# Turning the normed rows of two token tiles from SBUF, and storing them turned

## The chip, the cores and the metric

The kernel runs on one NeuronCore of a Trainium2 chip. Its engines each run their own instruction stream in order: TensorE (PE, with its weight loads shown as PEld), VectorE (DVE), ScalarE (ACT), GpSimd (POOL) and SyncE (SP). DMA transfers are issued in this kernel from SP's and from ACT's streams (SPq and ACTq in the profile). The metric is the device time of one launch in microseconds (us); lower is better.

## The reference

The reference is one decoder layer in float32 on 2048 tokens of width 1024:

```
hn   = rms_norm(x, mix_pre_g);  proj = hn @ w_in            # q, k, v and the conv input
attn = sliding_window_attention(q, k, v)                     # window 128, 8 heads, sinks, bias
conv = swish(layer_norm(depthwise31(glu(u)))) @ w_conv_pw
h    = x + rms_norm(concat(attn, conv) @ w_out, mix_post_g)
hn   = rms_norm(h, ffn_pre_g)
out  = h + rms_norm((silu(hn @ w_gate) * (hn @ w_up)) @ w_down, ffn_post_g)   # inner width 2816
```

The change concerns the second `hn`: the rows normed ahead of the feed-forward products. The rows lie with a token on each partition; the products need them turned, with a channel on each partition.

## The kernel before

**Tiles and stages.** Tokens are cut into four tiles (0 to 3) of 512. In the trace a buffer's name carries its stage and tile group behind an @: A is the input projection, B attention, C the convolution, U a folding of two weight matrices, W the output projection and both norms around the residual sum (four row blocks of 128 tokens in one tile), H the making of the feed-forward operands, F the gate and up products, G the down product. Tiles 0 and 1 go through H, F and G as one pair, tiles 2 and 3 as another; each pair is multiplied by a scheme of seven block products in place of eight, so H makes seven operands for a pair: B11 (tile 2i, channel blocks 0 to 3), B21 (the same tile, blocks 4 to 7), B22, and the sums T1 to T4. Every float32 operand is split in a high part (a cast by ACT, or by `split_f` at L792) and a low part (a subtraction on DVE or POOL), and each product takes three matmuls of the parts.

**The step that is changed.** `norm_w` (L747) ends a W stage. It adds the residual, stores h, and then an ACT pass per row block writes the normed rows into the buffers `xs` (tag "chl", five buffers, 4 KB a partition), which ACT's queue stores to the DRAM tensor `hn_scr` (L783). `load_cols` (L786) later reads from there, for one channel block k, the four 128x128 blocks of a tile, in pieces of 512 bytes; `turned` (L806) turns them on PE by four transposes against the identity (L810) into one bank of PSUM. `stage_h_plain` (L824) makes B11 and B21 in this way for tiles 0 and 2: an ACT pass with the gain from the bank (`ct`, one bank) to a buffer of tag "gb" (two buffers; L830), a store of it to `hT` by ACT's queue (L831), an ACT cast (L833) and a DVE subtraction. `stage_h_sums` (L837) reads `hT` again, and the columns of tiles 1 and 3 from `hn_scr`, for the other five operands.

**What sets the order.** The main line of the program is a generator run by `run`; beside it lanes (`lb`, `lc`, `lw`, `lh`, `lf` and others) hold generators for other stages. Each yield states an estimated time, and the lanes advance by that time and their rates. The order in which instructions are written is their priority; a planner with a simulated timeline of its own then fixes each engine's order and the buffers, and an instruction whose inputs are ready in that simulation can be put far ahead of the place where it was written. On the chip every engine keeps that fixed order. `lh` holds B11 and B21 of tile 0 (`stage_h_plain`), then tile 1's norm, then the sums. `until(name)` writes out the rest of a lane up to that name at once. `stage_w` (L693) for tile 1 computes the first half of its channels, then runs eight F products (`ready`), loads its second group of operands (`acts(gi + 1)`, four tiles of tag "chl", cast at L708) after the fourth of them, and goes on. For the second pair, `lw` holds C2, W2, C3, W3 and B11.2 in turn, beside the G stage of the first pair.

Of the kernel before, what the change touches and what calls it, by code (L numbers as in the profile page):

```python
# [12 lines left out]
F32 = mybir.dt.float32  # L13
# [4 lines left out]
AF = mybir.ActivationFunctionType  # L18
# [7 lines left out]
P = 128  # L26
T = 512
NT = S // T
KC = D // P
# [8 lines left out]
def layer_kernel(ctx, tc, x, xT, cols, rows, sinks, relb, onehot, w_in, w_pw, w_out, w_gate, w_up, w_down, out):  # L38
    nc = tc.nc
# [4 lines left out]
    dr = ctx.enter_context(tc.tile_pool(name="dr", bufs=1, space=DRAM))  # L44

    uid = [0]
    lab = ["X0"]
# [7 lines left out]
    def t_(tag, shape, dt=F32):  # L55
        return sb.tile(list(shape), dt, tag=tag, name=nm(tag), bufs=BUFS[tag])

    def f4(tag, shape=(P, D)):
        return t_(tag, shape)

    def f2(tag, shape=(P, T)):
        return t_(tag, shape)

    def hl(tag):
        return t_(tag, (P, 2, T), F32R)

    def sm(n, dt=F32):
        kind = "A" if lab[0][0] == "G" else lab[0][0]
        return sb.tile([P, 8], dt, tag="sm" + kind, name=nm("sm"), bufs=16)[:, 0:n]

    def bank(tag, bufs):
        return ps.tile([P, T], F32, tag=tag, name=nm(tag), bufs=bufs)
# [3 lines left out]
    ct = lambda: bank("ct", 1)  # L76


    act = nc.scalar.activation
# [54 lines left out]
    def weight(src, low, made, raw=None, on_pool=True):  # L134
        if raw is None:
            raw = t_("raw", (P, 2, T))
            nc.sync.dma_start(raw, src)
        return [split_w(raw[:, n], "w", low[n], made, on_pool) for n in range(2)]
# [5 lines left out]
    def rsqrt(ssq, n, mean_over, beside_taps=True):  # L144
        v = sm(n)
        y = sm(n)
        t = sm(n)
        vts(v, ssq, 1.0 / mean_over, EPS, ALU.mult, ALU.add)
        vts(y.bitcast(I32), v.bitcast(I32), 1, None, ALU.logical_shift_right)
        vts(y.bitcast(I32), y.bitcast(I32), -1, 0x5F3759DF, ALU.mult, ALU.add)  # L150
        for _ in range(3):
            if beside_taps:
                ptt(t, y, y, ALU.mult)
                ptt(t, t, v, ALU.mult)
                nc.gpsimd.tensor_scalar(t, t, -0.5, 1.5, ALU.mult, ALU.add)
                ptt(y, t, y, ALU.mult)
            else:
                vtt(t, y, y, ALU.mult)
                stt(t, v, -0.5, t, ALU.mult, ALU.mult)
                stt(y, t, 1.5, y, ALU.add, ALU.mult)  # L160
        return y
# [32 lines left out]
    ident = cst.tile([P, P], F32, name="ident")  # L194
# [16 lines left out]
    g_ffn = colt[:, 8:16]  # L211
# [29 lines left out]
    glu_scr = dr.tile([4, P, S], F32, name="glu_scr")  # L241
    hn_scr = dr.tile([S, D], F32, name="hn_scr")
    y_scr = dr.tile([4, P, S], F32, name="y_scr")
    qs = {}
    started = set()

# [433 lines left out]
    def block_half(acc, units, n, first, L, bank_of, s0=0):  # L680
        cs = slice(n * T, (n + 1) * T)
        for i in range(len(acc)):
            s = i + s0
            lab[0] = L
            o = bank_of()
            three(o, [((a[s // 4][:, 0, ss(s)], a[s // 4][:, 1, ss(s)]), (w[:, 0], w[:, 1])) for a, w in units])
            if first:
                act(acc[i][:, cs], o, AF.Copy)
            else:
                vtt(acc[i][:, cs], acc[i][:, cs], o, ALU.add)  # L690
            yield 0.65 * len(units)

    def stage_w(w, atag, htags, rtags, bank_of, norm=None, ready=None):  # L693
        G = KC // len(htags)
        L = f"W{w}"
        lab[0] = L
        acc = [f4(atag) for _ in range(4)]

        def acts(gi):
            aa = []  # L700
            lab[0] = L
            n = 4 if rtags[gi] == "yt" else 2
            for c in range(G * gi, G * gi + G, n):
                ms = t_(rtags[gi], (P, n, T))
                nc.sync.dma_start(ms, mixT[c : c + n, :, w * T : (w + 1) * T].rearrange("c p t -> p c t"))
                for j in range(n):
                    a = hl(htags[gi])
                    act(a[:, 0], ms[:, j], AF.Copy)  # L708
                    vtt(a[:, 1], ms[:, j], a[:, 0].bitcast(F32), ALU.subtract)
                    aa.append([a])  # L710
            return aa

        def weights(gi, n):
            ws = []
            for c in range(G * gi, G * gi + G, 2):
                if c < 4:
                    ws += weight(w_out[c : c + 2, :, n * T : (n + 1) * T].rearrange("c p t -> p c t"), lo_out[n, c : c + 2], w > 0, on_pool=False)
                else:
                    for j in range(2):
                        ws.append(hl("w"))  # L720
                        nc.sync.dma_start(ws[-1].bitcast(F32), fold[n, c - 4 + j])
            return ws

        nxt = acts(0)
        yield W_LEAD
        for gi in range(KC // G):
            aa = nxt
            for n in range(2):
                lab[0] = L
                if n == 1 and gi + 1 < KC // G and not (ready and G * gi + G == 4):  # L730
                    nxt = acts(gi + 1)
                ws = weights(gi, n)
                yield from block_half(acc, list(zip(aa, ws)), n, gi == 0, L, bank_of)
            if ready and G * gi + G == 4:
                for i, c in enumerate(ready()):
                    if i == Q0 // 2:
                        ld.until("C1")
                        lab[0] = L
                        nxt = acts(gi + 1)
                    yield c  # L740
        tail = norm_w(w, acc)
        if norm:
            norm(tail)
        else:
            yield from tail

    def norm_w(w, acc):  # L747
        L = f"W{w}"
        lab[0] = L

        def whole(src):
            t = f4("chl")
            nc.sync.dma_start(t, src)
            return t

        gb = whole(rows[0].partition_broadcast(P))
        ssq = sm(4)
        for s in range(4):
            act(junk, acc[s], AF.Square, accum_out=ssq[:, s : s + 1])
            yield 0.75  # L760
            lab[0] = L
        r = rsqrt(ssq, 4, D, w < 3)
        xs = [whole(x[w * T + s * P : w * T + (s + 1) * P]) for s in range(4)]
        ssq2 = sm(4)
        yield 3
        for s in range(4):
            lab[0] = L
            stt(acc[s], acc[s], r[:, s : s + 1], gb, ALU.mult, ALU.mult)
            yield 1.25
            lab[0] = L  # L770
            vtt(acc[s], xs[s], acc[s], ALU.add)
            r0 = w * T + s * P
            nc.sync.dma_start(h_scr[r0 : r0 + P], acc[s])
            act(junk, acc[s], AF.Square, accum_out=ssq2[:, s : s + 1])
            yield 1.25
        lab[0] = L
        r2 = rsqrt(ssq2, 4, D, w < 3)
        yield 3
        for s in range(4):
            lab[0] = L  # L780
            act(xs[s], acc[s], AF.Copy, scale=r2[:, s : s + 1])
            r0 = w * T + s * P
            nc.scalar.dma_start(hn_scr[r0 : r0 + P], xs[s])  # L783
            yield 1.25

    def load_cols(w, k, tag):  # L786
        t = f2(tag, (P, 4, P))
        nc.sync.dma_start(t, hn_scr[w * T : (w + 1) * T, k * P : (k + 1) * P].rearrange("(s p) c -> p s c", p=P))
        return t
# [14 lines left out]
    COLTAG = {0: ["fc", "at", "fc", "at"], 2: ["fc", "at", "fc", "at"]}  # L804

    def turned(w, k, bank_of, tag):  # L806
        c = load_cols(w, k, tag)
        b = bank_of()
        for s in range(4):
            nc.tensor.transpose(b[:, s * P : (s + 1) * P], c[:, s], ident)  # L810
        return b
# [12 lines left out]
    def stage_h_plain(ws, ops, n, off):  # L824
        L = f"H{ws[0]}"
        for k in range(4):
            lab[0] = L
            b = turned(ws[0], k + off, ct, COLTAG[ws[0]][k] if ws[0] else "fa")
            u = f2("gb")
            act(u, b, AF.Copy, scale=g_ffn[:, k + off : k + off + 1])  # L830
            nc.scalar.dma_start(hT[ws[0] // 2][k + off], u)  # L831
            o = op_tile(ws, ops, n, k, {})
            act(o[:, 0], u, AF.Copy)  # L833
            lo(u, o, False)
            yield 2.0
# [500 lines left out]
    lh = Lane(1.2, 0)  # L1336
# [65 lines left out]
            hn_a[t + 1] += split_x(t + 1, xa[t + 1][0], xa[t + 1][2], range(4, KC))  # L1402
    lw.until("W0")
    mids = [dr.tile([7, NF // 2, P, T], F32, name=f"mids{i}") for i in range(2)]
    hT = [dr.tile([KC, P, T], F32, name=f"hT{i}") for i in range(2)]
    td = dr.tile([4, NF // 2, P, T], F32, name="td")
    keeps = [dr.tile([PRES[2 * i], P, T], F32, name=f"keeps{i}") for i in range(2)]
    ws, ops = (0, 1), {}
# [12 lines left out]
    ws, ops = (2, 3), {}  # L1421
# [76 lines left out]
```

## Time and profile before

| what | value |
|---|---|
| median of 3 runs (lowest, highest) | 1991.65 us (1988.4, 1992.08) |
| the profiled execution's own time; its span | 1988.67 us; 1986.6 us |
| PE, DVE, ACT, POOL busy | 97%, 73%, 48%, 17% of the span |
| instructions | 26669 |
| DMA | 454.56 MB, 229 GB/s mean over the span |

The profiled execution is 2.07 us longer than its span and 2.98 us shorter than the median run. Times in the rows are microseconds from the start of the span. A row of a timeline has a start, a duration, the engine, the line in the kernel, the operation, what it writes and reads, a count, and in square brackets how long the engine stood idle before it and what released it. Lines L85 and L94 are helpers through which all matmuls, and all DVE operations, go, so they are told apart by the names of what they write.

### The profile page before, as it was taken

The page shows a single profiled execution, that of the slowest core. Times are in us where ns is not written, and L with a number is a line of the kernel's source. Part 1 is how long each engine was busy: PE and PEld are TensorE (multiplying, and loading weights), DVE is VectorE, ACT ScalarE, POOL GpSimd, SP SyncE. Part 2 cuts the span into 40 slices and gives each one's busy share as a digit, 9 for nine tenths or more (in the row PEclk, how much of TensorE's full clock was granted, in tenths as well). Part 3 has the DMA queues.
Part 4 walks back from the last instruction along what each step waited for, and adds up shares of the span by engine and source line. Part 5 has one row for each costly group of instructions (what it writes and reads, how often), then busy time and mean ns, then how long its engine had stood idle before and what let it go on. Part 6 is the DMA issues. An engine that isn't in the chain of part 4 may idle for free.

```text
span 1986.6 us, 26669 instructions
## 1 busy us (share of the span) xinstructions
PE 1930.2 (97%) x8730; PEld 1542.3 (78%) x8730; DVE 1460.2 (73%) x2578; ACT 955.2 (48%) x1878; POOL 336.4 (17%) x415
## 2 busy tenths in 40 slices
PE   8999999998999999899999999989999999999997
PEld 6777767776777778778888778768888888888886
DVE  5999969986875898888658975766666665455557
ACT  5455454436737633334355466556634433345443
POOL 4011111003121200000000110144423332311003
PEclk9999999999999999999999999989999999999999
DMA  8797757669659867885477788797844542466664
GB/s 312 253 316 234 228 176 242 213 198 306 203 191 353 290 216 237 285 267 181 154 236 251 266 302 282 270 315 244 289 149 165 170 164 81 143 232 194 210 196 144
DMA packets 229403, 454.56 MB, mean 229 GB/s; under 512 B 22632, under 2 KB 48400, under 8 KB 229264
## 3 DMA queue, kind: packets, MB, share of 16 engines
q1 hardware_dynamic: 211024, 426.64, 64.5%
q10 hardware_dynamic: 18240, 26.22, 3.6%
q8 instruction: 69, 1.13, 0.2%
q14 instruction: 70, 0.57, 0.1%
HBM read 331.65 MB, written 121.12 MB: 228 GB/s over the span
## 4 chain that ended last, share of the span: by engine, by line
PE 43%; DMA 10%; DVE 9%; issue 3%; POOL 2%; ACT 2%; SPq 1%; DVEq 0%; ACTq 0%; POOLq 0%
PE mm@F L85 29%; PE mm@G L85 12%; DVE fc@C L94 2%; PE tr@W L85 2%; DMA gb@F<-keeps 1%; DVE hl@G L94 1%; DMA mids<-fa@F 1%; DMA fa@G<-mids 1%; DMA td<-fc@G 1%; DVE w@F L94 1%; DMA fc@G<-w_down 1%; DMA wx@G<-w_down 1%; DVE fa@F L94 1%; DVE chl@F L94 1%; DMA mixT<-fc@C 1%
## 5 line engine op out<-in xcount | busy, mean ns | idle before, releaser
L94 DVE SCALAR_TENSOR_TENSOR fc@C<-glu@C,colt,fc@C 128x512 f32<-128x512 f32 x480 | 356.5, 760 | 2.9
L85 PE MATMUL mm@F<-hl@H,w@F 128*128 128x512 f32 x1056 | 253.0, 390 | 3.3 <-ACT mm@F L919 2.0
L85 PE MATMUL mm@G<-hl@G,hl@G 128*128 128x512 f32 x924 | 232.6, 397 | 11.2 <-ACT hl@G L792 7.7
L85 PEld LDWEIGHTS mm@F<-hl@H,w@F 128*128 128x128 f32 x1056 | 197.5, 188 | 46.3 <-ACT mm@F L919 3.7
L85 PEld LDWEIGHTS mm@G<-hl@G,hl@G 128*128 128x128 f32 x924 | 173.0, 190 | 51.7 <-ACT hl@G L792 9.0
L85 PE MATMUL mm@A<-hl@A,w@A 128*128 128x512 f32 x840 | 206.5, 395 | 4.2 <-ACT w@A L127 1.9
L792 ACT ACTIVATE w@F<-chl@F 128x512 fp32r<-128x512 f32 x220 | 135.4, 625 | 142.1 <-PE mm@F L85 131.5
L85 PE MATMUL mm@G<-w@G,hl@G 128*128 128x512 f32 x876 | 199.4, 389 | 0.0
L85 PEld LDWEIGHTS mm@G<-w@G,hl@G 128*128 128x128 f32 x876 | 164.4, 188 | 34.1
L85 PEld LDWEIGHTS mm@A<-hl@A,w@A 128*128 128x128 f32 x840 | 155.4, 188 | 42.2 <-ACT w@A L127 2.6
L94 DVE TENSOR_TENSOR w@F<-chl@F,w@F 128x512 fp32r<-128x512 f32 x198 | 144.8, 735 | 35.9 <-ACT w@F L792 35.3
L85 PE MATMUL mm@F<-ql@H,w@F 128*128 128x512 f32 x528 | 128.4, 391 | 9.2 <-ACT mm@F L1026 5.0
L85 PE MATMUL mm@F<-mid@H,w@F 128*128 128x512 f32 x528 | 131.7, 396 | 0.0
L85 PE MATMUL mm@F<-p@H,w@F 128*128 128x512 f32 x528 | 129.4, 390 | 0.0
L85 PE MATMUL mm@F<-x@H,w@F 128*128 128x512 f32 x528 | 125.7, 391 | 0.0
L85 PEld LDWEIGHTS mm@F<-ql@H,w@F 128*128 128x128 f32 x528 | 98.8, 188 | 31.6 <-ACT mm@F L1026 6.4
L494 POOL TENSOR_SCALAR_AFFINE_SELECT p@B<-p@B 128x512 f32<-128x512 f32 x62 | 57.6, 938 | 374.0 <-ACT p@B L492 372.7
L85 PEld LDWEIGHTS mm@F<-mid@H,w@F 128*128 128x128 f32 x528 | 100.0, 190 | 21.9 <-ACT fa@F L1047 0.5
L85 PEld LDWEIGHTS mm@F<-p@H,w@F 128*128 128x128 f32 x528 | 99.5, 188 | 21.0 <-ACT at@F L1040 0.2
L85 PEld LDWEIGHTS mm@F<-x@H,w@F 128*128 128x128 f32 x528 | 98.6, 188 | 21.5 <-issue 0.8
L127 ACT ACTIVATE w@A<-raw@A 128x512 fp32r<-128x512 f32 x110 | 67.4, 625 | 93.5 <-PE mm@A L85 54.8
L94 DVE TENSOR_TENSOR w@G<-raw@G,w@G 128x512 fp32r<-128x512 f32 x73 | 51.5, 705 | 68.1 <-ACT w@G L792 66.8
(302 smaller groups left out, 3300.6 us busy)
## 6 DMA issues: line engine op xcount, KB each, us to landing
mids<-fa@F SPq DMA_DIRECT2D x154, 256.0 KB, 2.8
raw@A<-w_in SPq DMA_DIRECT2D x55, 512.0 KB, 4.7
w@A<-lo_in SPq DMA_DIRECT2D x84, 256.0 KB, 3.6
fc@G<-mids SPq DMA_DIRECT2D x77, 256.0 KB, 3.5
fa@G<-mids SPq DMA_DIRECT2D x75, 256.0 KB, 4.6
gb@F<-keeps SPq DMA_DIRECT2D x72, 256.0 KB, 3.9
w@W<-fold SPq DMA_DIRECT2D x32, 512.0 KB, 5.1
chl@F<-w_gate SPq DMA_DIRECT2D x22, 512.0 KB, 4.1
```

The source lines that it names most:

```text
L85: r = nc.tensor.matmul(*args, **kw)
L94: r = op(*args, **kw)
L127: act(w[:, 0], raw, AF.Copy)
L494: nc.gpsimd.affine_select(out=pg[:, kb].rearrange("p (i q) -> p i q", q=P), in_=pg[:, 1].rearrange("p (i q) -> p i q", q=P), compare_op=AL ...
L792: act(w[:, 0], x, AF.Copy)
```

## The change

For tiles 0 and 2 the normed rows no longer go to `hn_scr`. A new function `turn_row(w, xs, k)` turns channel block k straight from the four buffers `xs`, applies the gain into a "gb" buffer and stores that to `hT`. For tile 0, `xs` is kept in the list `normed`, and `stage_h_plain` calls `turn_row` where it used to load and turn. For tile 2, `norm_w` calls it for all eight blocks as its last step, each with a yield of 2.0, and `stage_h_plain` only loads the turned blocks back from `hT` by SP's queue, into the buffers (tags "fc" and "at") that took the columns before. Ahead of the second group of tile 1's operands stands `lh.until("B21.0")`, since these take the "chl" buffers that `xs` now holds until it is turned. Tiles 1 and 3 keep the way through `hn_scr`.

```
@@ declarations
+    hT = [dr.tile([KC, P, T], F32, name=f"hT{i}") for i in range(2)]     # moved up
@@ stage_w
                     if i == Q0 // 2:
                         ld.until("C1")
+                        lh.until("B21.0")
                         lab[0] = L
                         nxt = acts(gi + 1)
@@ norm_w, last loop and behind it
             act(xs[s], acc[s], AF.Copy, scale=r2[:, s : s + 1])
-            r0 = w * T + s * P
-            nc.scalar.dma_start(hn_scr[r0 : r0 + P], xs[s])
+            if w % 2:
+                r0 = w * T + s * P
+                nc.scalar.dma_start(hn_scr[r0 : r0 + P], xs[s])
             yield 1.25
+        if w == 0:
+            normed.extend(xs)
+        if w == 2:
+            for k in range(KC):
+                turn_row(w, xs, k)
+                yield 2.0
+
+    normed = []
+
+    def turn_row(w, xs, k):
+        lab[0] = f"H{w}"
+        b = ct()
+        for s in range(4):
+            nc.tensor.transpose(b[:, s * P : (s + 1) * P], xs[s][:, k * P : (k + 1) * P], ident)
+        u = f2("gb")
+        act(u, b, AF.Copy, scale=g_ffn[:, k : k + 1])
+        nc.scalar.dma_start(hT[w // 2][k], u)
+        return u
@@ stage_h_plain
-            b = turned(ws[0], k + off, ct, COLTAG[ws[0]][k] if ws[0] else "fa")
-            u = f2("gb")
-            act(u, b, AF.Copy, scale=g_ffn[:, k + off : k + off + 1])
-            nc.scalar.dma_start(hT[ws[0] // 2][k + off], u)
+            if ws[0]:
+                u = f2(COLTAG[ws[0]][k])
+                nc.sync.dma_start(u, hT[ws[0] // 2][k + off])
+            else:
+                u = turn_row(0, normed, k + off)
+                lab[0] = L
             o = op_tile(ws, ops, n, k, {})
             act(o[:, 0], u, AF.Copy)
             lo(u, o, False)
```

More of the change, by code (lines that the diff above doesn't have):

```diff
@@ L1404, in layer_kernel @@
     mids = [dr.tile([7, NF // 2, P, T], F32, name=f"mids{i}") for i in range(2)]
-    hT = [dr.tile([KC, P, T], F32, name=f"hT{i}") for i in range(2)]
     td = dr.tile([4, NF // 2, P, T], F32, name="td")
```

## The prediction

> **What bounds the kernel now.** I read the page's busy shares first, then PE's waits over the whole span, then timelines and windows round the two waits that the change can reach.
>
> ```profile
> PE 1930.2 (97%) x8730; PEld 1542.3 (78%) x8730; DVE 1460.2 (73%) x2578; ACT 955.2 (48%) x1878; POOL 336.4 (17%) x415
> PE mm@G L85 <- ACT hl@G L792: 7.7, 3, 6.5
> PE tr@B L85 <- DVE sm@B L454: 5.6, 1, 5.6
> PE mm@F L85 <- ACT mm@F L1026: 5.0, 2, 3.8
> PE mm@F L85 <- ACT w@F L792: 4.0, 1, 4.0
> ```
>
> PE is busy for 1930.2 of 1986.6 us. The change takes no matmul away, so it can only win from the 56.4 us in which PE stands, and from time at a lowered clock. The two longest single waits, 6.5 and 5.6 us, both lie beside transfers that the change removes.
>
> Gap 1, at 486 us, in the timeline and in windows (columns: window, length, busy time of PE, PEld, DVE, ACT, POOL, then granted clock, DMA share, GB/s):
>
> ```profile
> 476.66 0.38 SPq L607 DMA_DIRECT2D mixT<-fc@C  x1
> 476.84 0.34 ACTq L783 DMA_DIRECT2D hn_scr<-chl@W  x1
> 480.59 0.67 ACTq L783 DMA_DIRECT2D hn_scr<-chl@W  x1
> 483.66 0.55 DVE L94 TENSOR_SCALAR fc@C<-glu@C,colt 128x512 f32<-128x512 f32 x1 [7.43 <-DMA mixT<-fc@C]
> 490.81 0.28 DVE L454 CUSTOM_DVE_ANT_0 p@B<-tr@B,mb@X 128x128 f32<-128x128 f32 x1
> 491.45 1.65 PE L85 MATMUL tr@B<-kz,ql@A 64*128 64x256 f32 x12 [5.59 <-DVE sm@B L454]
> 486.00:492.00 6.00, 0.55 (x4) 0.58 (x6) 5.96 (x18) 1.31 (x4) 0.00 (x0) 0.66 1.03 385
> 492.00:494.00 2.00, 2.00 (x14) 1.64 (x11) 1.96 (x4) 0.88 (x2) 0.00 (x0) 0.50 1.09 368
> 494.00:496.00 2.00, 2.00 (x8) 1.59 (x7) 2.00 (x5) 0.00 (x0) 0.00 (x0) 0.81 1.16 297
> 496.00:498.00 2.00, 2.00 (x10) 1.68 (x9) 2.00 (x8) 0.00 (x0) 0.00 (x0) 1.00 0.30 77
> ```
>
> PE waits for DVE, and DVE is late because a small store, issued at 476.66, frees its buffer only at 483.66. The first and the last of four stores of normed rows (512 KB each) are issued within 4 us of it; the DMA engines are full (share 1.03). After the gap the clock is 0.50 and 0.81 for two windows.
>
> Gap 2, at 1312 us:
>
> ```profile
> 1306.06 0.45 SPq L1102 DMA_DIRECT2D chl@G<-h_scr  x1
> 1308.79 0.67 ACT L830 ACTIVATE gb@H<-ct@H,colt 128x512 f32<-128x512 f32 x1
> 1315.01 0.33 ACTq L831 DMA_DIRECT2D hT<-gb@H  x1
> 1315.38 0.63 ACT L1094 ACTIVATE junk<-p@G 128x512 bf16<-128x512 f32 x1 [5.92 <-DMA chl@G<-h_scr]
> 1317.14 0.61 ACT L792 ACTIVATE hl@G<-mb@G 128x512 fp32r<-128x512 f32 x1
> 1318.33 8.49 PE L85 MATMUL mm@G<-hl@G,hl@G 128*128 128x512 f32 x24 [6.50 <-ACT hl@G L792]
> 1318.30:1320.30 2.00, 1.97 (x5) 1.60 (x6) 2.00 (x3) 2.00 (x5) 2.00 (x2) 0.50 1.08 330
> 1320.30:1322.30 2.00, 2.00 (x6) 1.57 (x5) 1.97 (x4) 1.97 (x7) 1.83 (x4) 0.50 0.69 165
> 1322.30:1324.30 2.00, 2.00 (x6) 1.59 (x5) 1.93 (x4) 1.40 (x4) 2.00 (x4) 0.53 0.86 261
> ```
>
> ACT has the last turned block of tile 2 ready at 1309.46 (1308.79 + 0.67). Its queue issues the store of it only at 1315.01, when another transfer, issued by SP at 1306.06, has landed. ACT stands behind its own store for 5.55 us, and the splits that PE needs stand behind ACT.
>
> **The change part by part.**
>
> *Tile 0, transfers.* Four stores and eight column loads leave (each 2 MB in all), with 3.99 us of SP's queue for the first four loads. The same small store lands elsewhere in 3.8 us:
>
> ```profile
> DMA to landing us min/median/max: 2.3/3.8/5.6
> 489.15 3.99 SPq L788 DMA_DIRECT2D fa@H<-hn_scr  x4
> 478.79 1.14 ACT L781 ACTIVATE chl@W<-x@W,sm@W 128x1024 f32<-128x1024 f32 x1
> 500.72 0.33 PE L810 MATMUL ct@H<-ident,fa@H 128*128 128x128 f32 x1
> 503.95 0.62 ACT L708 ACTIVATE chl@W<-yt@W 128x512 fp32r<-128x512 f32 x1
> 544.94 0.60 PE L810 MATMUL ct@H<-ident,fa@H 128*128 128x128 f32 x4
> 560.17 2.66 PE L85 MATMUL mm@W<-w@W,chl@W 128*128 128x512 f32 x11
> ```
>
> (The first row is for the buffers fc@C from 1100 to 1400 us.) With 3.8 us in place of 7.00, DVE and then PE go on 3.2 us sooner, and the gap shrinks to 2.4 us. The clock windows cost 2 x 0.50 + 2 x 0.19 + 0.55 x 0.34 = 1.6 us of PE's work; I take them as saved too. Term: -4.8 us. Bounds: 0, since DVE is busy throughout the gap (5.96 of 6 us) and the transfers that remain may hold the store as long, and -7.2 (the gap whole, 5.6 + 1.6), which turns of the rows put into the gap would also reach.
>
> *Tile 0, order.* The rows are ready at 479.9, and the turns need not wait for 500.72, so they come sooner; PE, full from 492 on, gains nothing by that. What waits instead: the casts into "chl" (503.95) must now come behind the last turn, at 544.94 if the turns do not move. That leaves 15 us to their first use at 560.17, where four casts of 0.62 us stand ahead. Cost 0; if that cover went, 4 x 0.62 = 2.5 us. The line that writes B21 out early costs nothing as long as the lane is done by then: 16 us of yields at rate 1.2 against 24.8 us of the main line's before it.
>
> *Tile 2, gap 2.* The store at 1315.01 moves away with the block that it carries, as do the last two turns and gain passes. ACT could then go on at 1309.46 and split 5.55 us sooner, leaving PE 0.95 of the 6.50 us. The clock loss after the gap (three windows at 0.50, 0.50 and 0.53, 2.9 us) would go as well: -8.45 us. DMA is still full there, and the next loads are late next: I give 2 us back. Term: -6.5 us. Bounds: 0 and -9.4 (6.5 + 2.9).
>
> *Tile 2, the new place.* Eight turns, eight gain passes and eight stores come behind the norm of tile 2, at about 1175 us, in place of four stores:
>
> ```profile
> 1163.42 0.63 ACT L792 ACTIVATE hl@G<-fa@G 128x512 fp32r<-128x512 f32 x1
> 1170.41 2.19 ACT L781 ACTIVATE chl@W<-mid@W,sm@W 128x1024 f32<-128x1024 f32 x2 [6.36 <-POOL sm@W L156]
> 1175.16 0.63 ACT L792 ACTIVATE hl@G<-mb@G 128x512 fp32r<-128x512 f32 x1 [0.48 <-ACT chl@W L781]
> 1176.37 1.53 PE L85 MATMUL mm@G<-hl@G,hl@G 128*128 128x512 f32 x4 [0.60 <-ACT hl@G L792]
> 1170.00:1180.00 10.00, 9.34 (x40) 7.17 (x39) 4.11 (x8) 9.11 (x14) 0.38 (x1) 1.00 0.82 288
> 1180.00:1190.00 10.00, 9.64 (x44) 7.45 (x43) 5.33 (x10) 5.20 (x10) 0.00 (x0) 1.00 0.94 314
> 1190.00:1200.00 10.00, 10.00 (x45) 8.18 (x45) 3.22 (x11) 5.15 (x9) 2.37 (x12) 1.00 0.89 318
> 1220.00:1240.00 20.00, 20.00 (x95) 16.55 (x94) 12.91 (x21) 13.41 (x25) 0.00 (x0) 1.00 0.92 303
> ```
>
> Here ACT makes no split from 1164.05 to 1175.16, first waiting 6.36 us for the norm on POOL, and PE runs dry for 0.60 us: the lead is just used up. The 32 transposes (8 x 0.60 = 4.8 us of PE, by the row at 544.94) and eight passes (8 x 0.67 us of ACT) only move, so they count 0 over the span. New are two waits: PE's own, for the rows, where ACT alone waited, and those of ACT behind its stores, which hold "gb" and the bank. Lower bound 0: from 1220 to 1240, where two such turns stand today, PE is never idle at a DMA share of 0.92. Upper bound 6.36 + 5.55 = 11.9 us: the norm's wait whole, and one store's as at 1309.46. I take 4 us, nearer the low end, since PE's one dry spell here is 0.60 us and ACT can make up ground after 1180 (5.20 and 5.15 of 10 us busy).
>
> *Tile 2, loads.* SP issues eight loads of `hT` for eight of columns: the same count, 0. Behind a late one, G's loads would queue; the turned stores fall before 1210, so the loads that matter stand behind nothing new. Four "chl" buffers are held longer; ACT's stores and casts for tile 3 come later still, so 0.
>
> *Sum.* -4.8 - 6.5 + 4.0 = -7.3 us on the profiled execution: 1988.67 - 7.3 = 1981.4. The median run was 2.98 us above that one, so for the median I predict 1984.4.
>
> **A rule beside the rows.** The Trainium skill (TensorE: Matmul & The Clock Gate, Part 1: The HAM clock gate) says that PE falls to half its clock after about one idle window of 3.4 us and needs about as long a busy one to return. The two gaps agree: 5.59 and 6.50 us, clock 0.50 behind both. By that rule the 4 us of the new place, as one piece, would add a loss of clock, to be weighed as a rival below; the sum leaves it out.
>
> The Trainium skill (DMA: Bandwidth & Descriptors, Rules for kernel authors) asks for transfers of 1 MiB or more. It speaks against eight stores of 256 KB for four of 512 KB; by it the DMA share at 1170 to 1200 would rise, and the sum come out higher by an unknown part.
>
> **The rivals.**
>
> *ACT's stores at the new place decide (slower).* ACT is busy 9.11 + 5.20 + 5.15 = 19.5 of the 30 us there; eight passes make 24.8, so about 5 us of store waits are free. The change gains 11.3 us elsewhere; it turns slower once the eight stores wait more than 16 us together, 2.0 us each. Store 1315.01 waited 5.55 us. At 3 us each (24 us) PE loses 19 in place of 4: 1984.4 + 15 = 1999. Against it: the windows to 1240 show such stores without a PE wait. Chance 0.24.
>
> *The planner orders something else anew (slower).* New buffer times shift its order downstream; a new wait like those of 3.8 and 4.0 us in the list, twice, with half clock of 1.6 us each, costs 11 us: 1995.8. No row speaks for a place. Chance 0.10.
>
> *Hidden.* DVE's backlog keeps gap 1, and full DMA keeps most of gap 2: half of 11.3 is gained, 4 to 5.5 lost, 1990 to 1992. The same comes out when the new wait is in one piece with a clock loss of 2.9 us and gap 2 keeps 2 us more. Chance 0.13.
>
> *More.* Turns fill what is left of gap 1, gap 2 goes whole, the new place costs nothing: -7.2 - 8.45 = -15.7, 1976. Chance 0.16.
>
> **How the numbers follow.** The forecast has 0.37. A change within 0.2% (4 us) cannot be told from none. Faster: 0.37 + 0.16 = 0.53; same 0.13; slower 0.24 + 0.10 = 0.34. The range must reach both slower cases and nearly the largest gain: 1976 to 2000. The forecast's own range, with 0 to 8 us at the new place, is 1980.4 to 1988.4.
>
> **What would show it.** Right: the stores of rows at 476 us are gone, the small store beside them lands in about 4 us, PE's wait on DVE near 486 is under 3 us with the clock at 1.00 behind it; the wait on the splits near 1312 is under 2.5 us and no ACT store waits there. Wrong: a PE wait over 4 us on the turned bank or on splits between 1165 and 1210, ACT idle ahead of several stores of turned rows, or a gap at 1312 that stays because the split's loads land late.

## The result, and the profile after

The changed kernel takes 2013.98 us (median of 4 runs, 2009.12 to 2014.5) against 1990.84 us for the kernel before in the same comparison. The ratio is 1.0121, with a 95% interval of 1.0107 to 1.0134: it is 1.2% slower, outside the predicted range and on the other side of no change. Its profiled execution took 2014.5 us, with a span of 2012.8 us; the figures below are of that execution, against the span of 1986.6 us of the one before.

The busy shares on the page of the changed kernel:

```profile
PE 1939.7 (96%) x8730; PEld 1549.3 (77%) x8730; DVE 1468.8 (73%) x2578; ACT 952.8 (47%) x1878; POOL 337.4 (17%) x415
```

PE does the same 8730 matmuls and is busy 9.5 us longer, so part of the loss is time at a lower clock (a mean of 0.987 in place of 0.992); it stands still for 73.1 us in place of 56.4. The waits of PE over the whole span (total, times, longest):

```profile
PE mm@F L85 <- ACT mm@F L942: 14.7, 6, 4.1
PE mm@F L85 <- DVE w@F L94: 5.9, 3, 3.5
PE mm@F L85 <- ACT w@F L813: 5.5, 2, 4.0
PE mm@F L85 <- ACT mm@F L1049: 5.1, 3, 3.1
```

The two waits that headed the list before, 6.5 us in G and 5.6 us in B, are both gone. All that heads the list now lies in F, and the largest group waits for "seeds": blocks that ACT casts into the product's bank (L942) after a load from `keeps`.

Where the time went is read from the starts of the same matmul in both traces:

| matmul | before | after | after - before |
|---|---|---|---|
| first F product of tile 0 with "x" | 521.9 | 512.3 | -9.6 |
| 265th F product with "hl" | 721.8 | 722.3 | +0.6 |
| first of G, first pair | 1013.0 | 1016.8 | +3.9 |
| 576th of G | 1223.7 | 1230.1 | +6.4 |
| last of G, first pair | 1342.7 | 1334.2 | -8.5 |
| 265th F product with "x" (second pair) | 1443.2 | 1469.5 | +26.3 |
| last of G with "w", second pair | 1971.1 | 1997.4 | +26.3 |

So 9.6 us are won at the first gap and lost again by 722 us; 15 us are won between 1224 and 1334 us; and 34.8 us are lost in the 100 to 135 us behind that. From 1470 us on the two kernels run alike.

**The first gap.** A window of the changed kernel in its place (columns as in the prediction):

```profile
486.00:492.00 6.00, 6.00 (x27) 4.89 (x28) 6.00 (x15) 3.70 (x7) 0.00 (x0) 1.00 0.73 237
```

PE is busy all through at full clock. What it does there, in the timeline of the changed kernel:

```profile
481.96 0.55 DVE L94 TENSOR_SCALAR fc@C<-glu@C,colt 128x512 f32<-128x512 f32 x1 [6.08 <-DMA mixT<-fc@C]
485.29 1.15 ACT L709 ACTIVATE hl@W<-yt@W 128x512 fp32r<-128x512 f32 x2 [2.28 <-DMA yt@W<-mixT]
486.21 6.65 PE L85 MATMUL mm@W<-w@W,hl@W 128*128 128x512 f32 x28
491.72 0.08 DVE L455 DVE_READ_ACCUMULATOR2_ANT sm@B<- 128x1 f32 x1
494.85 0.97 PE L85 MATMUL tr@B<-kz,ql@A 64*128 64x256 f32 x12
```

and the rows that answer to three of them in the timeline of the kernel before:

```profile
490.69 2.19 ACT L708 ACTIVATE hl@W<-yt@W 128x512 fp32r<-128x512 f32 x4 [4.69 <-DMA yt@W<-mixT]
491.01 0.08 DVE L454 DVE_READ_ACCUMULATOR2_ANT sm@B<- 128x1 f32 x1
493.03 7.45 PE L85 MATMUL mm@W<-w@W,hl@W 128*128 128x512 f32 x28
```

DVE still waits 6.08 us for the small store, and what B needs of DVE comes at 491.72, no earlier than before. PE no longer stands for it, and two things have changed. Tile 1's first W operand, a load of 1 MB that was issued among the stores of normed rows, now lands 5.1 us after its issue (480.18 to 485.27) and not 10.1 us (480.55 to 490.67), so it can be cast at 485.29 in place of 490.69. And the planner has put PE's work in another order: the 28 W matmuls stand ahead of the next twelve of B (494.85), where in the kernel before they stood behind them (491.45, then 493.03). Since PE keeps its fixed order, the earlier load alone would have left it standing for B; which of the two is worth how much, no run separates.

**Tile 2's new place, and C3.** Groups from the views of single buffers: count, shortest, median and longest in ns, and the starts of the first and the last in us. Before:

```profile
L549 PE MATMUL ct@C<-ident,fc@C x16: 270/272/300, 1125.4 to 1187.5; 128*128 128x128 f32 x16
L85 PE MATMUL tr@W<-w@W,chl@W x96: 389/389/397, 1238.7 to 1265.5; 128*128 128x512 f32 x96
L781 ACT ACTIVATE chl@W<-mid@W,sm@W x4: 1133/1135/1154, 1293.4 to 1296.5; 128x1024 f32<-128x1024 f32 x4
```

After (from the views of the buffers: tile 2's turns, what ACT's gain passes waited for, the landing of their stores, and the three rows that answer to those above):

```profile
L801 PE MATMUL ct@H<-ident,chl@W x32: 270/272/330, 1176.0 to 1219.1; 128*128 128x128 f32 x32
...
  PE ct@H L801: 5.5, 5
...
DMA to landing us min/median/max: 2.8/4.2/7.3
...
L550 PE MATMUL ct@C<-ident,fc@C x16: 270/272/273, 1224.4 to 1242.7; 128*128 128x128 f32 x16
L85 PE MATMUL tr@W<-w@W,chl@W x96: 389/389/389, 1297.7 to 1324.2; 128*128 128x512 f32 x96
L783 ACT ACTIVATE chl@W<-mid@W,sm@W x4: 1135/1136/1153, 1350.5 to 1353.6; 128x1024 f32<-128x1024 f32 x4
```

Tile 2's eight turns stand in the one bank `ct` from 1176.0 to 1219.1. C3's four column turns, which go through the same bank and stood at 1125 to 1187, come only behind them, at 1224. With C3 all that needs it is late: the second half of W3 by 59 us (1238.7 to 1297.7) and the normed rows of tile 3 by 57 us (1293.4 to 1350.5). The new stores themselves are harmless: they land in 4.2 us, and the only idle time of ACT ahead of the eight gain passes is for PE's turns, 5.5 us in all.

**What that costs.** Windows before:

```profile
1300.00:1340.00 40.00, 32.59 (x136) 25.52 (x135) 29.70 (x45) 17.93 (x40) 20.64 (x31) 0.87 0.93 314
1360.00:1400.00 40.00, 40.00 (x180) 33.03 (x179) 18.85 (x31) 23.43 (x43) 15.23 (x12) 1.00 0.90 302
1400.00:1440.00 40.00, 40.00 (x185) 32.97 (x184) 31.28 (x41) 26.52 (x48) 18.46 (x13) 1.00 0.85 286
```

and after:

```profile
1300.00:1340.00 40.00, 40.00 (x178) 33.14 (x177) 23.95 (x40) 16.17 (x29) 4.86 (x3) 1.00 0.48 175
1360.00:1400.00 40.00, 30.14 (x116) 22.38 (x114) 29.09 (x52) 17.07 (x41) 19.79 (x23) 0.91 1.01 342
1400.00:1440.00 40.00, 29.45 (x104) 23.07 (x105) 30.58 (x35) 24.99 (x47) 22.12 (x16) 0.79 0.74 250
```

Before, PE stood 7.4 us of 1300 to 1340 and was full behind it. After, it is full there and stands 20.4 us of 1360 to 1440, at clocks of 0.91 and 0.79. In both kernels the bad stretch begins some 20 us behind tile 3's normed rows: PE's first wait of about 1 us or more starts 18 us after 1293.4 before, and 17 us after 1350.5 in the changed kernel. The waits of PE from 1340 to 1445 us, after:

```profile
PE mm@F L85 <- ACT mm@F L942: 9.5, 4, 3.3
PE mm@F L85 <- DVE w@F L94: 5.9, 3, 3.5
PE mm@F L85 <- ACT fa@F L964: 3.1, 2, 2.2
```

**The loss between 614 and 722 us.** Windows before, and then after:

```profile
620.00:640.00 20.00, 18.23 (x87) 14.59 (x85) 8.34 (x13) 13.53 (x23) 0.00 (x0) 1.00 1.02 359
```

```profile
620.00:640.00 20.00, 15.62 (x64) 12.68 (x64) 8.27 (x13) 11.16 (x20) 0.00 (x0) 0.83 1.02 356
```

PE comes there 8 us earlier (613.9 in place of 622.2 for the first F product with "hl"), and stands 4.06 us for the third seed, which ACT casts at 622.93, only 1.4 us earlier than before (624.34). At a mean clock of 0.83 in this window, more of the lead goes: it is 4.0 us at the 25th of these matmuls and 2.6 us at the 37th.

### The profile page after: what moved, and what is told of

It is laid out like the page before. It is cut to its first block, busy times and chain, and to the rows that moved or that the text cites. A ratio compares the mean times of both kernels' runs of the same rounds, so it can differ in the third digit from the quotient of the medians.

```text
span 2012.8 us, 26656 instructions
## 1 busy us (share of the span) xinstructions
PE 1939.7 (96%) x8730; PEld 1549.3 (77%) x8730; DVE 1468.8 (73%) x2578; ACT 952.8 (47%) x1878; POOL 337.4 (17%) x415
## 5 line engine op out<-in xcount | busy, mean ns | idle before, releaser
L85 PE MATMUL mm@G<-hl@G,hl@G 128*128 128x512 f32 x924 | 228.3, 393 | 3.6 <-DVE hl@G L94 2.4
L85 PE MATMUL mm@F<-mid@H,w@F 128*128 128x512 f32 x528 | 140.5, 414 | 18.0 <-ACT mm@F L942 9.5
L85 PEld LDWEIGHTS mm@F<-mid@H,w@F 128*128 128x128 f32 x528 | 105.2, 201 | 43.6 <-ACT mm@F L942 10.7
```

The source lines that it names most:

```text
L85: r = nc.tensor.matmul(*args, **kw)
```

## The experiments

Two questions: which part costs what, and why. For tile 2 three theories were set against each other. **Bank**, later **delay**: the eight turns take `ct` ahead of C3's turns, W3 and tile 3's norm come late, and this is what costs after 1360 us. **Lane**: C3 and W3 are late because the lane `lw` spends 16 units of time on the turns. **Store**: ACT's stores and the two "gb" buffers cost (the prediction's rival). All ratios are to the kernel before on the same chip; two profiles of one and the same kernel below differ by 4.6 us in their last matmul, all of it arisen after 722 us, so such differences of single profiles behind 722 us are not weighed.

**Each part alone.** Tile 0's part alone, against the changed kernel:

```
-            if w % 2:
+            if w:
                 r0 = w * T + s * P
                 nc.scalar.dma_start(hn_scr[r0 : r0 + P], xs[s])
...
-        if w == 2:
-            for k in range(KC):
-                turn_row(w, xs, k)
-                yield 2.0
...
             if ws[0]:
-                u = f2(COLTAG[ws[0]][k])
-                nc.sync.dma_start(u, hT[ws[0] // 2][k + off])
+                b = turned(ws[0], k + off, ct, COLTAG[ws[0]][k])
+                u = f2("gb")
+                act(u, b, AF.Copy, scale=g_ffn[:, k + off : k + off + 1])
+                nc.scalar.dma_start(hT[ws[0] // 2][k + off], u)
```

> Tile 0 as in the change, tile 2's rows and turns as before. Bank theory (all of the loss comes from tile 2's eight turns, which hold the one bank ct ahead of C3's column turns): the stall at 1312 us is back, nothing is lost after 1360 us, and what tile 0 gains at 486 us is given back by 720 us, since tile 1's norm ends at the same time as before; so 1990 to 1996 us, ratio 1.000 to 1.003. My prediction's tile 0 term (-4.8 us kept) gives 1986, ratio 0.9975. If tile 0's part were the cause of the loss: over 2005 us.

Measured: 1993.11 us, ratio 1.0042 (1.0025 to 1.0060). The stall in G is back, nothing is lost after 1360 us, and the 7.7 us won at the first gap have become a loss of 4.5 us at 722 us: tile 0's part costs by itself. The size of that loss varies: in the five kernels here that have tile 0's part and leave tile 1's roots on POOL, the product of 721.8 comes at 721.6 to 726.3. None of them keeps more than 0.2 us of the lead.

Tile 2's part alone, against the changed kernel:

```
-                        lh.until("B21.0")
...
-            if w % 2:
+            if w != 2:
...
-                u = turn_row(0, normed, k + off)
-                lab[0] = L
+                b = turned(0, k + off, ct, "fa")
+                u = f2("gb")
+                act(u, b, AF.Copy, scale=g_ffn[:, k + off : k + off + 1])
+                nc.scalar.dma_start(hT[0][k + off], u)
```

> Tile 2 as in the change, tile 0 as before. Bank theory: most of the 23 us of loss is here, 2005 to 2015 us, ratio 1.007 to 1.012, with the waits between 1360 and 1440 us that the changed kernel has. If the loss needs both parts: below 1996 us.

Measured: 2007.03 us, ratio 1.0093 (1.0073 to 1.0114). The two parts add up within their intervals: 0.42% and 0.93% against 1.21% for both. As the bank theory says, W3's second half comes at 1295.1 and from the end of G to the product that stood at 1443.2 before it takes 134.9 us in place of 100.5, a loss of 34.4 us.

**Other banks.** The whole change, with tile 2's turns in the three banks `tr`:

```
-        b = ct()
+        b = tr() if w else ct()
```

> The whole change with tile 2's eight turns in the three tr banks instead of ct; the lane's order and its 16 units of time, the gb buffers and ACT's stores stay. Bank theory: C3's first turns are back at some 1130 us, W3's second half at about 1240 us, the waits after 1360 us go: 1980 to 1992 us. Lane theory (C3 and W3 come later because the lane spends 16 units on the turns) and store theory (ACT's stores and the two gb buffers space the turns): the loss stays, 2005 to 2015 us. A cost that the bank theory does not count: W3's own products use tr too, and stand behind the turns there.

Measured: 1999.77 us, ratio 1.0059 (1.0039 to 1.0080), above the 1980 to 1992 us of the bank theory, and below what the other two expected. Its groups:

```profile
L801 PE MATMUL tr@H<-ident,chl@W x32: 270/272/328, 1175.3 to 1197.3; 128*128 128x128 f32 x32
L550 PE MATMUL ct@C<-ident,fc@C x16: 270/272/273, 1129.6 to 1191.8; 128*128 128x128 f32 x16
L783 ACT ACTIVATE chl@W<-mid@W,sm@W x4: 1135/1137/1152, 1303.9 to 1307.0; 128x1024 f32<-128x1024 f32 x4
```

C3's turns are back in their old place although lane time, stores and buffers are unchanged, and the loss behind G has gone (from the end of G to the product of 1443.2 it takes 102.3 us, 100.5 before, 135.3 in the changed kernel). What is left is tile 0's part (0.42% by itself) and the cost named beforehand: W3's first half now stands behind the turns in `tr` (it begins at 1199.0 in place of 1147.5), and G ends 10 us later than before, 4.3 us of which it had lost by its start.

The Trainium skill (Perfetto Trace Analysis, section Matmuls) advises rotating independent groups through several banks, so that emptying one overlaps the next group. The traces agree: the eight turns take 22.0 us in three banks and 43.1 us in one.

**Another place.** The whole change with the eight turns given out behind C3 in the same lane; bank, stores, buffers and the 16 units stay:

```
-        if w == 0:
-            normed.extend(xs)
-        if w == 2:
-            for k in range(KC):
-                turn_row(w, xs, k)
-                yield 2.0
+        if w % 2 == 0:
+            normed[:] = xs
...
+    def stage_turns():
+        for k in range(KC):
+            turn_row(2, normed, k)
+            yield 2.0
...
     lw.add("C3", stage_tail(3), lambda: since(lc, "T3", CS))
+    lw.add("H2t", stage_turns())
```

> The whole change with tile 2's eight turns given out in the same lane after C3's tail instead of before it; bank, buffers, stores and the 16 units stay. Bank theory: C3's first three turns come back to 1125 to 1140 us, tile 3's normed rows to about 1300 us, and the loss after 1360 us goes, at least 15 of the 23 us: 1980 to 1998 us. Lane theory: W3 stands behind the same 16 units, so the loss stays, 2005 to 2015 us. Store theory: the same eight stores in the same buffers, 2005 to 2015 us.

Measured: 2006.14 us, ratio 1.0090 (1.0069 to 1.0112); the profiled execution, 2000.39 us, is the fastest of its four. A miss in size for the bank theory: C3's turns did come back (1125.3 to 1181.4), but the time hardly fell. The turns now hold the "chl" buffers until 1266, W3's second half needs these, and all but the first 12 of its 96 matmuls come some 30 us late; tile 3's rows are at 1332.0, and the loss behind G is 24.2 us. So it is not C3's turns in themselves that cost, but what makes tile 3's norm late. From here on I speak of the delay theory.

**No lane time.** The whole change without the time that tile 2's turn loop hands in:

```
                 turn_row(w, xs, k)
-                yield 2.0
```

> The whole change without the 16 units of lane time that tile 2's turn loop hands in; bank, place and stores stay. Lane theory (C3 and W3 are late because the lane spends 16 units on the turns): C3's first turn at about 1130 us, and most of the loss goes, below 2000 us. Bank theory: the eight turns still stand ahead of C3's in the one bank, C3's first turn at 1215 us or later, and the time stays at 2005 to 2018 us.

Measured: 2006.18 us, ratio 1.0090 (1.0073 to 1.0107), with C3's first turn at 1226.4 and tile 3's rows at 1352.3. The lane theory falls: without the 16 units C3 is as late.

**The turns without the change.** The kernel before, with eight turns of tile 2's rows added at the changed kernel's place, their result copied and used by nothing:

```
             nc.scalar.dma_start(hn_scr[r0 : r0 + P], xs[s])
             yield 1.25
+        if w == 2:
+            for k in range(KC):
+                lab[0] = "H2"
+                b = ct()
+                for s in range(4):
+                    nc.tensor.transpose(b[:, s * P : (s + 1) * P], xs[s][:, k * P : (k + 1) * P], ident)
+                act(f2("gb"), b, AF.Copy, scale=g_ffn[:, k : k + 1])
+                yield 2.0
```

> The kernel before, with eight turns of tile 2's normed rows into ct added at the place where the change has them; each is copied to a gb buffer and not stored, and everything else stays, the way through DRAM too. Delay theory: C3's turns come some 45 to 55 us late, W3's second half about 59 us late, tile 3's normed rows at about 1350 us, and the waits between 1360 and 1440 us appear although nothing of tile 2's route has changed: 15 to 35 us above before. And the stall at 1312 us shrinks, if tile 3's norm is what fills that time in the kernel before; it stays at 6 us and more, if it is tile 2's way through DRAM. Store theory (the new stores to hT decide): no store is added, so within 5 us of before.

Measured: 2007.27 us, ratio 1.0107 (1.0078 to 1.0137). Its groups, and its windows:

```profile
L549 PE MATMUL ct@C<-ident,fc@C x16: 270/272/273, 1218.7 to 1237.0; 128*128 128x128 f32 x16
L781 ACT ACTIVATE chl@W<-mid@W,sm@W x4: 1132/1135/1154, 1342.9 to 1346.1; 128x1024 f32<-128x1024 f32 x4
```

```profile
1300.00:1340.00 40.00, 40.00 (x186) 33.02 (x185) 25.56 (x48) 22.44 (x41) 5.72 (x4) 1.00 0.62 226
1360.00:1400.00 40.00, 28.40 (x110) 22.09 (x109) 27.83 (x55) 19.63 (x44) 22.46 (x32) 0.83 1.03 363
```

This kernel stores nothing turned early and sends tile 2's rows through DRAM as ever, yet it loses some 22 us, in the same place. The store theory falls. And the stall of 1300 to 1340 us is gone here too, with tile 2's way through DRAM untouched: that way alone does not make the stall. Tile 3's norm has moved off, and the DMA share of that stretch is 0.62 in place of 0.93.

**Tile 2 without the delay.** Tile 2's part alone, the turns in `tr` and inside W3, behind its first quarter and ahead of the loads that want "chl" (against the kernel with tile 2's part alone):

```
             for n in range(2):
                 lab[0] = L
+                if w == 3 and n == 1 and gi == 0:
+                    for k in range(KC):
+                        turn_row(2, normed, k)
+                        yield 2.0
+                    lab[0] = L
...
         if w == 2:
-            for k in range(KC):
-                turn_row(w, xs, k)
-                yield 2.0
+            normed[:] = xs
+
+    normed = []
...
-        b = ct()
+        b = tr() if w else ct()
```

> Tile 2's part alone (tile 0 as before), its eight turns moved once more: in the three tr banks, and given out inside W3, behind the first of its four quarters and ahead of the loads that want the chl buffers. C3's turns then stand ahead of them, W3's first quarter too. Delay theory (the loss after 1360 us comes only from C3 and W3 being late, so that tile 3's norm falls into pair 2's first products): C3's turns at 1125 to 1190 us, W3's second half at 1235 to 1250 us, no loss after 1360 us beyond 3 us; as to the stall at 1312 us: if it is tile 2's way through DRAM it goes and the time is 6 to 8 us below before (1977 to 1982 at 1985 of before); if it is tile 3's norm and its transfers, it stays and the time is within 4 us of before. If the new stores or turns cost by themselves, wherever they stand: 10 us and more above before.

Measured: 1987.22 us against 1985.71 us, ratio 1.0005 (0.9987 to 1.0023): all of tile 2's loss is gone, and no gain is left. Its rows, windows, and PE's waits over 1 us from 1240 to 1345 us:

```profile
L787 ACT ACTIVATE chl@W<-mid@W,sm@W x4: 1134/1136/1137, 1289.7 to 1292.8; 128x1024 f32<-128x1024 f32 x4
```

```profile
1300.00:1340.00 40.00, 35.35 (x160) 28.28 (x159) 28.63 (x45) 18.84 (x41) 19.82 (x31) 1.00 0.94 318
1360.00:1400.00 40.00, 40.00 (x180) 33.06 (x179) 17.30 (x29) 23.58 (x43) 13.34 (x10) 1.00 0.89 300
1271.99 0.73 PE L85 MATMUL mm@G<-hl@G,hl@G 128*128 128x512 f32 x2 [3.24 <-DVE hl@G L94]
1305.65 11.16 PE L85 MATMUL mm@G<-hl@G,hl@G 128*128 128x512 f32 x48 [2.88 <-DVE x@G L94]
1327.10 3.24 PE L85 MATMUL mm@G<-hl@G,hl@G 128*128 128x512 f32 x13 [1.67 <-DVE hl@G L94]
```

Tile 3's rows are on time, and the F products are full again. The one wait of 6.50 us behind ACT's store is gone together with that store. The four other profiles that keep tile 2's way through DRAM and tile 3's norm on time (tile 0's part alone, and below the same with roots on DVE, twice, and its control) all have it, at 5.77 to 6.13 us. But PE stands as long in sum, 8.4 us from 1240 to 1345 as before, at other waits. For the first, 3.24 us, DVE is busy with tile 3's norm (4.86 us of scaling from 1266.47); the second, 2.88 us, goes back to a load of `w_down` for which ACT waits until 1301.74. From the first to the last G product of the pair it takes 328.9 us, before 329.7 us.

Eight kernels in one table; the last column is the time from the last G matmul of the first pair to the product at 1443.2 before:

| kernel | tile 3's rows normed at | PE idle 1240 to 1345 | PE idle 1345 to 1460 | G's end to F |
|---|---|---|---|---|
| before | 1293.4 | 8.4 | 0.0 | 100.5 |
| tile 2's turns in `tr`, inside W3 | 1289.7 | 8.4 | 1.0 | 101.9 |
| whole change, turns in `tr` | 1303.9 | 7.0 | 1.6 | 102.3 |
| whole change, turns behind C3 | 1332.0 | 3.3 | 15.8 | 124.7 |
| before, with eight idle turns | 1342.9 | 0.0 | 19.0 | 133.0 |
| tile 2's part alone | 1347.9 | 0.0 | 20.7 | 134.9 |
| changed kernel | 1350.5 | 0.0 | 20.4 | 135.3 |
| whole change, no lane time | 1352.3 | 0.0 | 18.5 | 126.7 |

With tile 3's norm late, G stands less and F stands more, and F loses more than G wins. The lateness sets the size only roughly: the last kernel has the latest rows and loses 8.6 us less behind G than the changed kernel.

**Tile 0.** Its win at the first gap is gone by 722 us. In the run with tile 0's part alone, POOL's timeline shows the first inverse root of tile 1's norm mixed with the masks of attention:

```profile
584.95 0.68 POOL L153 TENSOR_TENSOR sm@W<-sm@W 128x4 f32<-128x4 f32 x1 [7.27 <-DVE sm@W L94]
...
588.80 1.67 POOL L495 TENSOR_SCALAR_AFFINE_SELECT p@B<-p@B 128x512 f32<-128x512 f32 x2
...
595.07 0.20 POOL L156 TENSOR_TENSOR sm@W<-sm@W,sm@W 128x4 f32<-128x4 f32 x1
```

It takes 10.3 us, where the kernel before takes 5.0 (593.88 to 598.89), and ends only 3.6 us earlier although it began 8.9 us earlier. So I put both roots of tile 1 on DVE, in the kernel with tile 0's part and, as a control, in the kernel before:

```
-        r = rsqrt(ssq, 4, D, w < 3)
+        r = rsqrt(ssq, 4, D, w in (0, 2))
...
-        r2 = rsqrt(ssq2, 4, D, w < 3)
+        r2 = rsqrt(ssq2, 4, D, w in (0, 2))
```

> Tile 0's part alone, and tile 1's two inverse roots on DVE instead of POOL. Norm theory (the 8 us that tile 0 wins at 486 us are lost at 620 to 720 us because tile 1's norm does not end earlier: its roots took 10.3 us on POOL in place of 4.8 us): the norm's casts come 4 to 9 us earlier than in the run with tile 0's part alone, the seeds behind them too, and the time is 4 to 8 us below that run's. Rival (the transfers are at their limit from 600 to 640 us, share 1.03, and set the pace): the casts come earlier and the time is the same within 2 us.

> The control for the run before: the kernel before with tile 1's two inverse roots on DVE instead of POOL. In the kernel before the roots are done 4.8 us after they start, so both theories expect the same time as before within 3 us; what it differs by is to be taken off the effect in the run with tile 0's part.

Measured: 1982.62 us, ratio 0.9984 (0.9967 to 1.0001), with tile 0's part; 1991.94 us, ratio 1.0027 (1.0015 to 1.0040), for the control. The edit costs 0.3% in the kernel before, where no change was expected, and wins 0.6% with tile 0's part, some 11 us. That is more than the 4 to 8 us of the norm theory, and the way is not the one that it named: the norm's casts begin at 614.9 in place of 617.2, 2.3 us earlier and not 4 to 9. In the changed kernel, with the roots on POOL, they begin at 614.87 too, and the lead is lost all the same. In ACT's timeline of this run a seed stands right behind the casts:

```profile
618.08 1.13 ACT L783 ACTIVATE chl@W<-mid@W,sm@W 128x1024 f32<-128x1024 f32 x1
...
619.12 0.58 ACT L940 ACTIVATE mm@F<-gb@F 128x512 f32<-128x512 f32 x1
```

With the roots on POOL this seed comes at 625.3, behind five more passes and a table load. The new order wins 6 us there, PE waits 0.97 us in place of 4.48, and the order is new because the planner reckons with another engine for the roots. The product of 721.8 comes at 715.6 here, so some 6 us of the lead are kept. That the roots' time on POOL is the cause is therefore not shown; the timelines point to ACT's order of seeds around tile 1's norm, and no run changes that order alone.

The same kernel again, in more rounds:

> The same kernel as tile 0's part alone with tile 1's roots on DVE, measured again in more rounds: 0.9984 of before again, within 0.2%; over 1.000 if the first run's gain was the spread of the runs.

Measured: 1986.10 us against 1988.50 us, ratio 0.9989 (0.9976 to 1.0001): the same again, and no more than a tenth of a percent faster than before.

**The change with one repair, and with both.** The whole change with tile 1's roots on DVE (the edit above, in the changed kernel):

> The whole change as it is, with tile 1's roots on DVE. If tile 0's loss (some 10 us between its part with POOL roots and with DVE roots) and tile 2's loss (the ct bank) are separate, the ratio to before is 1.0121 - 0.0055 = 1.006 to 1.008, some 2000 us at 1986 of before; if the later loss swallows what is won earlier, 1.010 and more.

Measured: 2007.81 us, ratio 1.0100 (1.0084 to 1.0117), where the second expectation begins: the repair for tile 0 wins 0.2% here and not 0.55%. In its profile, that of the fastest of its four runs (2003.67 us), the lead at the end of G is 19.4 us, against 8.5 in the changed kernel, and the loss in F is 34.0 us as ever; what of the lead the other runs keep isn't known.

Both repairs in the changed kernel, the turns in `tr` inside W3 and the roots on DVE, each by the edit shown above:

> Both tiles' turns as the change wants them, with the two costs found so far taken out: tile 2's eight turns in the tr banks inside W3 (as in the run where tile 2 alone was so moved) and tile 1's roots on DVE. If the two parts add up, tile 0's part with DVE roots (0.9984) and tile 2's moved part (1.0005) give 0.999, within 0.3% of before; if tile 2's part had a gain of its own that only the delay of C3 and W3 hid, 6 us and more below before (ratio under 0.997).

Measured: 1980.71 us against 1988.50 us, ratio 0.9967 (0.9954 to 0.9980). This version beats both kernels: 0.33% faster than before, and some 1.5% faster than the change as made. It is 0.22% below the kernel with tile 0's part and DVE roots alone, while tile 2's moved part alone was 0.05% above before; whether tile 2's part wins anything of its own stays open within these 0.2%: the ratio meets both expectations, 0.999 within 0.3% and under 0.997.

## Why the prediction was wrong

**Tile 0, transfers (-4.8, bounds 0 and -7.2).** The gap closed and the clock stayed at 1.00, as said; the win at 521.9 was 9.6 us, beyond the bounds. That the gap closed was luck, for the mechanism was another: the store landed in 5.5 us (476.30 to 481.8), not 3.8, DVE's wait went from 7.43 to 6.08 us, and B's sums came no earlier. What helped was a load that I had not looked at, tile 1's W operand among the stores, cast 5.4 us earlier, and a new order on PE that puts its products ahead of B's. I had asked only what PE waited for, not what else could have run.

**Tile 0, order (0).** This step failed. "PE, full from 492 on, gains nothing by that" left out the way on: what is won must be kept through the next place where other work sets the time. At 619.5 us PE, 8.3 us early, met a seed that ACT cast only 1.4 us earlier than before, and stood 4.06 us for it. Tile 0's part costs 0.42% by itself.

**Tile 2, gap 2 (-6.5, bounds 0 and -9.4).** This step failed in what it took the wait to be worth. The reading of the wait itself holds: where the store has moved away, no wait on ACT's splits of that length is left, and where it stays and tile 3's norm is on time, there is one of 5.77 to 6.13 us. But with tile 3 on time, PE stands the same 8.4 us at other waits, for DVE and for a late load; the prediction gave back 2 us for that. Nor does the store alone make the wait: with tile 2's way through DRAM kept and tile 3's norm late, it goes. So the term is about 0. In the changed kernel G is faster because tile 3's norm has left it; the eight added turns alone do the same.

**Tile 2, the new place (+4.0, bounds 0 and 11.9).** For the place itself the size is about right: PE waited 1.94 us for the first turn, at a clock of 1.00, and lost 2.5 us between 1013 and 1224 us. The sum failed here all the same, and this is the step that made it wrong: it priced the eight turns by PE's and ACT's time and not by the one bank that they hold. "Only move, so they count 0" is true of PE's time and false of `ct`: 43 us of it, ahead of C3 by the order of writing. It delayed tile 3's norm by 57 us and cost 34.8 us in F, of which G gives back some 15: the standing that is gone, a clock of 1.00, and turns that stand elsewhere. I had asked what is late next for SP's loads and for "chl", and not for the bank.

**Tile 2, loads (0).** As said; the "chl" buffers cost nothing in the changed kernel, though they did when the turns were put behind C3.

**The rivals.** The slower one, ACT's stores at the new place, had the right sign and the wrong mechanism: no store was waited for, and eight turns without a store cost the same. Nearest came "the planner orders something else anew"; I gave it 0.10 and 11 us (by its own terms 1995.4, not 1995.8) because no row spoke for a place. There was one: C3's turns in the same bank at 1125 to 1187 us, ahead of the place of the new ones in time and behind it in the order of writing.

**The signs.** None of the signs that were to show the prediction wrong came, and of those that were to show it right only the store's landing failed (5.5 us in place of about 4). They watched the places of the change, and the loss came in F, behind 1360 us.

**The two rules.** By the clock rule that the prediction takes from the Trainium skill (TensorE: Matmul & The Clock Gate, Part 1: The HAM clock gate), a wait of 4 us in one piece at the new place would have cost clock. It was 1.94 us, and the clock stayed at 1.00 from 1170 to 1200. By the rule on transfer size that it takes from the Trainium skill (DMA: Bandwidth & Descriptors, Rules for kernel authors), the DMA share at 1170 to 1200 would have risen. It was 0.45, 0.79 and 0.91, against 0.82, 0.94 and 0.89; only four of the eight stores are issued in these 30 us, so this is a weak test.

**What stays open.** Why the same norm costs F some 35 us and G only some 15 is not settled. The transfers are at their limit from 1360 to 1400 (share 1.01), F's first products need loads of weights and seeds at that time, and the waits are for seeds and weights; ACT's longest wait there, 7.85 us up to 1396.0, ended when a load of weights landed. But no run separates the transfers from the order on ACT and DVE.

## What to carry to other kernels

Price moved work by every resource that it holds, a single bank or buffer ahead of all, and look up who takes that resource next in the order in which the program gives it out, not in the order of the trace. A wait that goes away in the profile is not yet time won: other waits can take its place, or it went for another reason. Add the new work alone, and take the old work away alone. A few microseconds won early are kept only if the next meeting point with another queue moves as well, so follow the lead from stage to stage before it is counted.

## What the runs showed of the hardware

The clock fell without a wait as long as those at the two gaps. Windows of the changed kernel:

```profile
1368.00:1372.00 4.00, 2.58 (x10) 1.80 (x10) 1.76 (x6) 1.31 (x4) 0.24 (x2) 1.00 1.03 385
1372.00:1376.00 4.00, 2.57 (x6) 2.11 (x7) 3.05 (x7) 2.20 (x8) 3.62 (x6) 0.69 0.97 342
```

PE waited 0.98 us up to 1368.6 and 2.20 us up to 1373.4, and no longer wait had come in F of the second pair until then. The 0.69 is a mean: in windows of 1 us the granted clock is 1.00 up to 1373, 0.50 from 1374 to 1376, and 1.00 again from 1377. The Trainium skill (TensorE: Matmul & The Clock Gate, Part 1: The HAM clock gate) gives in its table of states one idle window of about 3.4 us as the condition. Here waits of 0.98 and 2.20 us within 6 us were enough, so waits of that length are to be reckoned with clock as well. It is not so each time: behind the wait of 1.94 us at 1176.0 the clock stayed at 1.00.

Small POOL instructions of 128x4 took 0.20 us in the one case and 0.52 to 0.74 us in the other. Masks on the same engine are not what tells the two apart: in the kernel before the long ones come at 596.04 and 596.86 as well (0.74 and 0.58 us), where no mask runs. Spans on POOL are rough, so this is a reading and not a measurement.
